# A decoder layer on one core: rows of like TensorE instructions held together, ends of ada blocks issued later

## The chip, the cores and the metric

The program runs on one core of one Trainium2 chip. The metric is the device time of one execution, in microseconds (us), given as the median of several runs. All arithmetic on TensorE (PE) is in FP32 or in pairs of FP32R matmuls; VectorE (DVE), ScalarE (ACT) and GpSimd (POOL) work beside it, and SyncE (SP) issues the weight loads.

## The reference

One layer of a decoder (D = 2048, 256 prompt tokens, 8 x 4 sample tokens, 288 tokens in all):

```
mod = silu(c) @ w_ada + b_ada                    # 9 rows x 6 * 2048: shift, scale, gate, twice
h = rmsnorm(x, g_pre_mix) * (1 + sc_m) + sh_m
q, k, v, gu, gv = split(h @ w_in)                # 1024 | 128 | 128 | 1024 | 1024 columns
attn = sliding-window GQA with sinks and a T5 bias      # 16 heads, 2 kv heads, blocks of 128;
                                                 # sample tokens see a cache of 128 keys each
gmlp = gelu(gu) * (tril(w_s) @ rmsnorm(gelu(gv)) + b_s) # 8 heads, chunks of 128
x = x + gt_m * rmsnorm(concat(rmsnorm(attn), rmsnorm(gmlp)) @ w_out)
h = rmsnorm(x, g_pre_ff) * (1 + sc_f) + sh_f
x = x + gt_f * rmsnorm(square(relu(h @ w_ff1)) @ w_ff2)
```

Outputs are x, the new rows of k and v, and the normalised v rows of the gMLP.

## The kernel before

Activations lie transposed: 128 channels on the partitions, 288 tokens in the columns, 16 such blocks (k = 0..15) for D. Each is kept as a high and a low part (xh, xl), and a weight unit that SP has loaded into a `raw` buffer (five buffers, one queue, one unit after another) is split into h (ACT, L321) and l (DVE, L322). A product is then three matmuls of 128x288 on the full 128 by 128 array: xh by h, xl by h, xh by l (L336, L337, L340; L485, L486, L488 for w_in; L924 for slabs of w_out and w_ff1).

The ada product has nine rows only. It is done in FP32 straight from the raw unit: four matmuls, each of the nine columns of silu(c) against 512 columns (256 or 128 in narrow blocks), stand in four 32-column strips of the array (L363), so four consecutive ones can run beside each other: a pack. In the profile an FP32 matmul leaves two records, a pack of four eight records. A wide block takes four units of one pack each, then its end: ACT copies the sums to `adS` (L367), PE turns it with four transposes (L375), DVE reduces and stores it (L377 to L387).

Other small work on parts of the array: scores of a pair of heads (L531, L532, 64 rows each), the three transposes of the probabilities (L567) and P V of the pair (L572 with 256 and L575 with 128 columns, 64-column halves, two run as a pack), for sample tokens the scores against the cache (L604, eight of 64x32 per kv set), the transposes (L631, L632) and P V (L638, L643), in the gate the transposes of gv (L675, L676) and two products per head (L730, L731).

`items` is a list of work in the order of the program: Win groups of w_in with ada units between; the last group with attention, sample attention and the start of the gate (`do`, at a priority raised by HP = 50 positions); the o slab with the gates; w_out's other units (Main) with groups of three ada units; the residual with norm (`resid`, raised by 60); the f1 slab; the feed-forward. A scheduler gives each engine its order: it takes the ready instruction of the highest priority, by its own estimate of when data is there. So instructions of one step can be pulled apart, and others slipped between. Before, nothing holds the matmuls of a step together. `behind(i, others)` adds a pure ordering to it. `na(n)` hands out the next n ada units in front of which a place in `items` stands, and takes a block's end along straight behind its last unit; `group`, for the later stretch, already puts off an end to the next group.

Of the kernel before, what the change touches and what calls it, by code (L numbers as in the profile page):

```python
# [19 lines left out]
KT = D // 128  # L20
NP = 256
NB = 8
NT_S = 4
NS = NB * NT_S
# [7 lines left out]
KG0 = tuple(sum(KG[:i]) for i in range(len(KG)))  # L32

HP = 50
GTAB = 1
LA, SA = 4, 1
TAILS = ((0, 2), (2, 2), (4, 2), (6, 4), (10, 3), (13, 2), (15, 1))
# [68 lines left out]
def build():  # L106
# [32 lines left out]
    with tile.TileContext(nc) as tc, ExitStack() as root:  # L139
# [10 lines left out]
        V, S, PE, G = nc.vector, nc.scalar, nc.tensor, nc.gpsimd  # L150
# [4 lines left out]
        def behind(ins, others):  # L155
            for o_ in others:
                tc.add_manual_dep(ins, o_.name, mybir.DependencyInfo(mybir.DependencyClass.NoSync,
                                                                     mybir.DependencyReason.DATA),
                                  reason="table order")

        def tracked(i):
            behind(i, order["prev"] if order["load"] is None else [order["load"]])
# [27 lines left out]
        ident = sm("ident")  # L190
# [8 lines left out]
        sc = cp.tile([128, KT, 32], F32, name="sc")  # L199
# [99 lines left out]
        class Unit:  # L299
            src = None  # L300
            cols = 2 * HALF
            n = HALF
# [43 lines left out]
        class Ada(Unit):  # L346
# [7 lines left out]
            def run(self):  # L354
                w, cw = self.w, 128 * self.w
                if self.i == 0:
                    st["ada", self.blk] = pa.tile([128, 512], F32, name="ada")
                ps = st["ada", self.blk]
                nk = KT // w
                for kk in range(nk):  # L360
                    k = self.i * nk + kk
                    g = 32 * (k % 4)
                    PE.matmul(ps[g:g + 32, :cw], sc[:, k], self.raws[:, kk * cw:kk * cw + cw], start=k < 4,  # L363
                              stop=k >= KT - 4, skip_group_check=True)
                if self.i == w - 1:
                    sb = cp.tile([128, 512], F32, name="adS", bufs=2)
                    S.copy(sb[:, :cw], ps[:, :cw])  # L367
                    st["ada", self.blk] = sb

        def ada_fin(blk):  # L370
            c, j0, w = blk
            sb = st["ada", blk]
            pt = pa.tile([128, 512], F32, name="ada")
            for q in range(w):
                PE.transpose(pt[:, q * 128:q * 128 + 128], sb[:, q * 128:q * 128 + 128], ident)  # L375
# [132 lines left out]
        vN = ap_.tile([128, 2, 128], F32, name="vN")  # L508
# [13 lines left out]
        def attn1(i):  # L522
# [2 lines left out]
            G.dma_start(bias[:, :, 0:128], bass.AP(er.tensor, i * EW, [[1, 128], [8 * EW, 2], [1, 128]]))  # L525
            L = bias
            kR = st["kR"]
            for hf in range(2):
                p0 = 64 * hf
                ps = pp.tile([128, 512], F32, name="ps")  # L530
                PE.matmul(ps[:, 0:128], at[p0:p0 + 64, i, 0:128], kR[p0:p0 + 64, 128:256], start=True, stop=True)  # L531
                PE.matmul(ps[:, 128:384], at[p0:p0 + 64, i, 128:256], kR[p0:p0 + 64, 0:256], start=True, stop=True)  # L532
# [27 lines left out]
        def attn2(i):  # L560
            L = st[i]
            pT = []
            for hf in range(2):
                pT.append(ap_.tile([128, 384], F32, name="pT", bufs=2))
                ps = pp.tile([128, 512], F32, name="ps")
                for q, to in ((0, 0), (2, 1), (1, 2)):
                    PE.transpose(ps[:, to * 128:to * 128 + 128], L[:, hf, q * 128:q * 128 + 128], ident)  # L567
                S.copy(pT[hf], ps[:, :384])
            po = pp.tile([128, 512], F32, name="ps")
            for hf in range(2):  # L570
                p0 = 64 * hf
                PE.matmul(po[p0:p0 + 64, 0:256], vN[:, 1, p0:p0 + 64], pT[hf][:, 0:256], start=True, stop=False)  # L572
            for hf in range(2):
                p0 = 64 * hf
                PE.matmul(po[p0:p0 + 64, 128:256], vN[:, 0, p0:p0 + 64], pT[hf][:, 256:384], start=False, stop=True)  # L575
            V.tensor_copy(at[:, i, 0:256], po[:, 0:256])

        def samp0(h):
# [7 lines left out]
        def samp1(h):  # L586

            ck = st["ck"]
# [5 lines left out]
            st["vS"] = vS  # L594
            L = sp.tile([128, 2, 144], F32, name="Ls", bufs=1)
            pss = [pp.tile([128, 512], F32, name="ps") for _ in range(2)]
            for kv in range(2):
                p0 = 64 * kv
                PE.matmul(pss[kv][:, 128:144], qS[p0:p0 + 64, 4 * h:4 * h + 4].rearrange("p b c -> p (b c)"),
                          kT[p0:p0 + 64, n0:n0 + 16], start=True, stop=True)  # L600
            for b in range(4):
                for kv in range(2):
                    p0 = 64 * kv
                    PE.matmul(pss[kv][32 * b:32 * b + 32, 0:128], qS[p0:p0 + 64, 4 * h + b], ck[p0:p0 + 64, b],  # L604
                              start=True, stop=True)
            for kv in range(2):
                V.scalar_tensor_tensor(L[:, kv], pss[kv][:, 0:144], 0.125, biasS[:, kv], ALU.mult, ALU.add)
# [17 lines left out]
        def samp2(h):  # L625
            L, cv, vS = st["Ls"], st["cv"], st["vS"]
            pT = sp.tile([128, 2, 128], F32, name="pTs", bufs=1)
            pN = sp.tile([16, 2, 128], F32, name="pNs", bufs=1)
            psT = pp.tile([128, 512], F32, name="ps").rearrange("p (a c) -> p a c", a=4)
            for kv in range(2):  # L630
                PE.transpose(psT[:, kv], L[:, kv, 0:128], ident)  # L631
                PE.transpose(psT[:16, 2 + kv], L[:, kv, 128:144], ident)  # L632
            S.copy(pT, psT[:, 0:2])
            S.copy(pN, psT[:16, 2:4])
            po = pp.tile([128, 512], F32, name="ps")[:, :128].rearrange("p (b c) -> p b c", b=4)
            for kv in range(2):
                p0 = 64 * kv
                PE.matmul(po[p0:p0 + 64].rearrange("p b c -> p (b c)"), vS[:, p0:p0 + 64], pN[:, kv], start=True,  # L638
                          stop=False, skip_group_check=True)
            for b in range(4):  # L640
                for kv in range(2):
                    p0 = 64 * kv
                    PE.matmul(po[p0:p0 + 64, b], cv[:, b, p0:p0 + 64], pT[:, kv, 32 * b:32 * b + 32], start=False,  # L643
                              stop=True, skip_group_check=True)
# [6 lines left out]
        gm = {}  # L651
# [19 lines left out]
        def gvnat(h):  # L671
            vG, vGs = gm["vG"], gm["vGs"]
            ps = pp.tile([128, 512], F32, name="ps")
            for q in range(2):
                PE.transpose(ps[:, q * 128:q * 128 + 128], gv[:, h][:, q * 128:q * 128 + 128], ident)  # L675
            PE.transpose(ps[:NS, 256:384], gv[:, h][:, NP:], ident)  # L676
# [48 lines left out]
        def gate(h):  # L725
            vG, vGs = gm["vG"], gm["vGs"]
            bs = gm["bs"][:, h]
            ps = pp.tile([128, 512], F32, name="ps")[:, :T]
            for q in range(2):
                PE.matmul(ps[:, q * 128:q * 128 + 128], vG[:, q, h], gm["ws"][:, h], start=True, stop=True)  # L730
            PE.matmul(ps[:, NP:], vGs[:, h], gm["wss"][:, h], start=True, stop=True)  # L731
            t = gv[:, h]
            V.scalar_tensor_tensor(t[:, :NP].rearrange("p (q c) -> p q c", q=2),
                                   ps[:, :NP].rearrange("p (q c) -> p q c", q=2), sm("gvg", h),
# [61 lines left out]
        adas = []  # L796
# [4 lines left out]
        for b in ADA_BLOCKS:  # L801
            if b[0] == 5:
                adas2 += ada_items(b)

        def na(n):
            out = []
            while adas and n > 0:
                it = adas.pop(0)
                out.append(it)
                n -= it.src is not None  # L810
            if adas and adas[0].src is None:
                out.append(adas.pop(0))
            return out

        last = [Win(pc) for pc in WIN_PIECES if pc[0] == len(KG) - 1]

# [152 lines left out]
        def ev_bo():  # L969
            for n in range(NO):  # L970
                ev_o(n)(bo[n][:, :T])

        late = []

        def group(src, n):

# [227 lines left out]
```

## Time and profile before

| | |
|---|---|
| median of 3 runs | 1317.36 us (1317.17 to 1321.53) |
| profiled execution | 1320.14 us, of it 1318.4 us are its span |
| PE busy | 1286.0 us, 98% |
| DVE, ACT, POOL busy | 735.3, 540.0, 36.1 us |
| L363 of 128x512 | 576 records, 76.1 us |
| PE waits for adS L367 / sums L1006 | 5.0 / 3.2 us |

Busy time is time in which at least one instruction of the engine is in flight; a matmul's end is modelled, and consecutive ones overlap, so what a piece of work costs PE is read from start to start. Records named xN are N instructions in a row. "128*32" is the part of the array that an instruction uses (rows by columns), "128x512" its moving operand. In order listings of the program the names carry buffer numbers, and "x3" counts instructions (one per FP32 matmul).

### The profile page before, as it was taken

To read this page: it belongs to the slowest core of one execution; us is meant where nothing else is said; L and a number is where in the kernel's file an instruction comes from. 1 tells how busy PE (TensorE), PEld (TensorE's weight loads), DVE (VectorE), ACT (ScalarE), POOL (GpSimd) and SP (SyncE) were. 2 spreads that over 40 slices of the span, in tenths; PEclk is the share of its full clock that TensorE was granted. 3 is DMA by queue.
4 is the path that set the end of the run, shared out by engine and by line. 5 is a ranking of instruction groups with operands and counts; after the bars stand their busy time and mean duration, and the time that the engine had idled before them with its cause. 6 is when DMAs were issued, how large, how long until landed. Compare 5 with 4: busy or idle time off the path is not lost.

```text
span 1318.4 us, 23358 instructions
## 1 busy us (share of the span) xinstructions
PE 1286.0 (98%) x9770; PEld 1177.8 (89%) x9770; DVE 735.3 (56%) x1407; ACT 540.0 (41%) x873; POOL 36.1 (3%) x59
## 2 busy tenths in 40 slices
PE   6999999999999999999999999999999999999997
PEld 5788886767788689999999889999999999999996
DVE  5888676667644696543334445444544444545554
ACT  4333234466323365443334333334443334444331
POOL 0210001211000000000000000000000000000000
PEclk9999999999999999999999999999999999999999
DMA  9888977677978775544446776445444445544411
GB/s 358 328 312 311 339 285 263 178 285 253 356 319 318 280 264 192 164 166 173 170 160 256 273 291 266 160 160 170 174 168 160 160 160 168 175 169 160 160 65 72
DMA packets 46010, 291.40 MB, mean 221 GB/s; under 512 B 5834, under 2 KB 6410, under 8 KB 15056
## 3 DMA queue, kind: packets, MB, share of 16 engines
q1 hardware_dynamic: 43344, 284.26, 58.6%
q0 software_dynamic: 2416, 5.47, 1.9%
q8 instruction: 76, 1.25, 0.4%
q14 instruction: 30, 0.25, 0.1%
q10 hardware_dynamic: 144, 0.18, 0.0%
HBM read 287.18 MB, written 2.70 MB: 220 GB/s over the span
## 4 chain that ended last, share of the span: by engine, by line
PE 60%; DVE 1%; ACT 0%; DVEq 0%; issue 0%
PE ps L336 20%; PE ps L340 20%; PE ps L337 19%; PE ada L363 1%; DVE acc L1086 0%; DVE x L1092 0%; PE ada L375 0%; PE ps L1083 0%; ACT nr L166 0%; PE ps L270 0%; PE ps L264 0%; DVE mn L214 0%; DVE mn L215 0%; DVE nr L216 0%; DVE mn L224 0%; DVEq L139 0%
## 5 line engine op out<-in xcount | busy, mean ns | idle before, releaser
L322 DVE TENSOR_TENSOR l<-raw,h 128x1024 fp32r<-128x1024 f32 (+3 forms) x368 | 416.3, 1140 | 294.0 <-ACT h L321 291.4
L321 ACT CAST h<-raw 128x1024 fp32r<-128x1024 f32 (+3 forms) x368 | 357.7, 984 | 500.5 <-PE ps L337 410.0
L336 PE MATMUL ps<-xh,h 128*128 128x288 f32 x1120 | 301.8, 297 | 1.7 <-ACT h L321 1.0
L337 PE MATMUL ps<-xl,h 128*128 128x288 f32 x1120 | 301.1, 295 | 0.0
L337 PE MATMUL ps<-fl,h 128*128 128x288 f32 x1024 | 276.9, 295 | 0.0
L336 PE MATMUL ps<-fh,h 128*128 128x288 f32 x1024 | 276.9, 298 | 0.0
L336 PEld LDWEIGHTS ps<-xh,h 128*128 128x128 f32 x1120 | 210.4, 188 | 7.0 <-ACT h L321 5.3
L337 PEld LDWEIGHTS ps<-xl,h 128*128 128x128 f32 x1120 | 211.6, 189 | 0.8 <-issue 0.8
L336 PEld LDWEIGHTS ps<-fh,h 128*128 128x128 f32 x1024 | 193.0, 188 | 0.0
L337 PEld LDWEIGHTS ps<-fl,h 128*128 128x128 f32 x1024 | 192.2, 188 | 0.0
L340 PE MATMUL ps<-xh,l 128*128 128x288 f32 x1120 | 171.7, 295 | 0.0
L340 PE MATMUL ps<-fh,l 128*128 128x288 f32 x1024 | 157.3, 296 | 0.0
L340 PEld LDWEIGHTS ps<-xh,l 128*128 128x128 f32 x1120 | 156.1, 188 | 0.0
L340 PEld LDWEIGHTS ps<-fh,l 128*128 128x128 f32 x1024 | 142.7, 188 | 0.0
L485 PE MATMUL ps<-xh,h 128*128 128x288 f32 x416 | 118.6, 308 | 4.3 <-ACT xh L292 2.3
L486 PE MATMUL ps<-xl,h 128*128 128x288 f32 x416 | 117.7, 301 | 0.0
L363 PE MATMUL ada<-raw,sc 128*32 128x512 f32 (+2 forms) x1088 | 104.4, 480 | 7.4 <-DMA raw<-wada 7.4
L485 PEld LDWEIGHTS ps<-xh,h 128*128 128x128 f32 x416 | 78.5, 192 | 18.5 <-issue 6.3
L488 PE MATMUL ps<-xh,l 128*128 128x288 f32 x416 | 87.2, 301 | 0.0
L486 PEld LDWEIGHTS ps<-xl,h 128*128 128x128 f32 x416 | 79.8, 192 | 2.6 <-issue 2.4
L363 PEld LDWEIGHTS ada<-raw,sc 128*32 128x32 f32 x1088 | 31.4, 112 | 44.8 <-issue 31.7
L488 PEld LDWEIGHTS ps<-xh,l 128*128 128x128 f32 x416 | 66.6, 192 | 1.1 <-issue 1.0
(255 smaller groups left out, 931.9 us busy)
## 6 DMA issues: line engine op xcount, KB each, us to landing
raw<-wada SPq DMA_DIRECT2D x96, 1024.0 KB, 7.4
raw<-f SPq DMA_DIRECT2D x64, 1024.0 KB, 4.8
raw<-f1B SPq DMA_DIRECT2D x58, 1024.0 KB, 4.8
raw<-woB SPq DMA_DIRECT2D x12, 1024.0 KB, 9.2
raw<-win SPq DMA_DIRECT2D x11, 1024.0 KB, 8.7
raw<-win SPq DMA_DIRECT2D x14, 640.0 KB, 4.8
raw<-f1A SPq DMA_DIRECT2D x8, 768.0 KB, 7.2
raw<-win SPq DMA_DIRECT2D x6, 768.0 KB, 5.9
```

The lines of the kernel that those rows point to most:

```text
L321: S.copy(h, rw)
L322: V.tensor_tensor(l, rw, h.bitcast(F32), ALU.subtract)
L336: PE.matmul(ps, w, self.mh[:, k], start=k == 0, stop=False)
L337: PE.matmul(ps, w, self.ml[:, k], start=False, stop=False)
L340: PE.matmul(ps, l[:, kk * 128:kk * 128 + 128], self.mh[:, k], start=False, stop=k == 15)
L363: PE.matmul(ps[g:g + 32, :cw], sc[:, k], self.raws[:, kk * cw:kk * cw + cw], start=k < 4, stop=k >= KT - 4, skip_group_check=True)
L485: PE.matmul(ps, w, xh[:, k0 + kk], start=kk == 0, stop=False)
L486: PE.matmul(ps, w, xl[:, k0 + kk], start=False, stop=False)
L488: PE.matmul(ps, l[:, o_ + kk * 128:o_ + kk * 128 + 128], xh[:, k0 + kk], start=False, stop=kk == s - 1)
```

## The change

A class Row is added. The first instruction of a row is issued as before; each later one is issued at a priority raised by 20000 positions and ordered behind the one ahead of it, so that once the first is placed, the rest follow at once. Rows are: the four matmuls of an ada unit (eight or sixteen in narrow blocks); the transposes of an ada end; the four score matmuls of a pair; the three transposes of each half; the four P V matmuls of a pair, with half 1 now ahead of half 0; the ten score matmuls of a sample set; its four transposes, small ones first; its ten P V matmuls; the three transposes of a gv head; the three matmuls of a gate. And `na` puts a block's end behind the units of its next call, as `group` does; `late` moves ahead of it.

```diff
+TOP = 20000
+        class Row:
+            prev = None
+
+            def __call__(self, f, *a, **kw):
+                if self.prev is None:
+                    i = f(*a, **kw).ins
+                else:
+                    with tc.high_priority(offset=TOP):
+                        i = f(*a, **kw).ins
+                    behind(i, [self.prev])
+                self.prev = i
+                return i
...
+                row = Row()
                 for kk in range(nk):
...
-                    PE.matmul(ps[g:g + 32, :cw], sc[:, k], self.raws[:, kk * cw:kk * cw + cw], start=k < 4,
-                              stop=k >= KT - 4, skip_group_check=True)
+                    row(PE.matmul, ps[g:g + 32, :cw], sc[:, k], self.raws[:, kk * cw:kk * cw + cw], start=k < 4,
+                        stop=k >= KT - 4, skip_group_check=True)
...
             po = pp.tile([128, 512], F32, name="ps")
-            for hf in range(2):
+            row = Row()
+            for hf in (1, 0):
                 p0 = 64 * hf
-                PE.matmul(po[p0:p0 + 64, 0:256], vN[:, 1, p0:p0 + 64], pT[hf][:, 0:256], start=True, stop=False)
-            for hf in range(2):
+                row(PE.matmul, po[p0:p0 + 64, 0:256], vN[:, 1, p0:p0 + 64], pT[hf][:, 0:256], start=True, stop=False)
+            for hf in (1, 0):
...
+            row = Row()
             for kv in range(2):
                 p0 = 64 * kv
-                PE.matmul(pss[kv][:, 128:144], qS[p0:p0 + 64, 4 * h:4 * h + 4].rearrange("p b c -> p (b c)"),
+                row(PE.matmul, pss[kv][:, 128:144], qS[p0:p0 + 64, 4 * h:4 * h + 4].rearrange("p b c -> p (b c)"),
                           kT[p0:p0 + 64, n0:n0 + 16], start=True, stop=True)
             for b in range(4):
                 for kv in range(2):
                     p0 = 64 * kv
-                    PE.matmul(pss[kv][32 * b:32 * b + 32, 0:128], qS[p0:p0 + 64, 4 * h + b], ck[p0:p0 + 64, b],
+                    row(PE.matmul, pss[kv][32 * b:32 * b + 32, 0:128], qS[p0:p0 + 64, 4 * h + b], ck[p0:p0 + 64, b],
...
+            row = Row()
             for q in range(2):
-                PE.matmul(ps[:, q * 128:q * 128 + 128], vG[:, q, h], gm["ws"][:, h], start=True, stop=True)
-            PE.matmul(ps[:, NP:], vGs[:, h], gm["wss"][:, h], start=True, stop=True)
+                row(PE.matmul, ps[:, q * 128:q * 128 + 128], vG[:, q, h], gm["ws"][:, h], start=True, stop=True)
+            row(PE.matmul, ps[:, NP:], vGs[:, h], gm["wss"][:, h], start=True, stop=True)
...
+        late = []
+
         def na(n):
-            out = []
+            out, ends = [], list(late)
+            late.clear()
             while adas and n > 0:
                 it = adas.pop(0)
-                out.append(it)
-                n -= it.src is not None
+                if it.src is None:
+                    ends.append(it)
+                else:
+                    out.append(it)
+                    n -= 1
             if adas and adas[0].src is None:
-                out.append(adas.pop(0))
-            return out
+                late.append(adas.pop(0))
+            return out + ends
```

What it does to PE's order, at three places. In the listings of after, L169 is the first instruction of a row and L172 any later one; the names tell what it is (ck, qS: sample scores; bias: transposes of probabilities; pT, vN: P V; raw, sc: ada; adS, ones: sums of squares; small, adS: transposes of an ada end).

The first place is the scores of the first sample set (about 212 us in the trace). PE before, where ps_2623 and ps_2624 are the two score tiles:

```order
L567 MATMUL ps_2652<-small_75,bias_2354 128x128 x3
L604 MATMUL ps_2623<-ck_654,qS_122 32x128
L567 MATMUL ps_2658<-small_75,bias_2354 128x128
L604 MATMUL ps_2624<-ck_654,qS_122 32x128
L567 MATMUL ps_2658<-small_75,bias_2354 128x128
L604 MATMUL ps_2623<-ck_654,qS_122 32x128
L567 MATMUL ps_2658<-small_75,bias_2354 128x128
L604 MATMUL ps_2624<-ck_654,qS_122 32x128
L572 MATMUL ps_2663<-pT_2651,vN_125 64x256
```

PE after:

```order
L172 MATMUL ps_2623<-ck_654,qS_122 32x128
L172 MATMUL ps_2624<-ck_654,qS_122 32x128
L172 MATMUL ps_2623<-ck_654,qS_122 32x128
L172 MATMUL ps_2624<-ck_654,qS_122 32x128
L172 MATMUL ps_2623<-ck_654,qS_122 32x128
L172 MATMUL ps_2624<-ck_654,qS_122 32x128
L172 MATMUL ps_2623<-ck_654,qS_122 32x128
L172 MATMUL ps_2624<-ck_654,qS_122 32x128
L169 MATMUL ps_2652<-small_75,bias_2354 128x128
L172 MATMUL ps_2652<-small_75,bias_2354 128x128 x2
L169 MATMUL ps_2658<-small_75,bias_2354 128x128
L172 MATMUL ps_2658<-small_75,bias_2354 128x128 x2
```

The eight cache scores now stand in a row behind the two of the new keys, and the six transposes behind them; before, transposes, P V and scores of a head pair came between.

The second place is ada units between the last attention pairs (about 250 us). PE before, where raw_3022 and raw_3079 are two units:

```order
L363 MATMUL ada_3170<-raw_3022,sc_95 32x512 x3
L363 MATMUL ada_3170<-raw_3079,sc_95 32x512
L572 MATMUL ps_3331<-pT_3319,vN_125 64x256
L531 MATMUL ps_3343<-kR_2347,at_121 128x128
L532 MATMUL ps_3343<-kR_2347,at_121 128x256
L531 MATMUL ps_3347<-kR_2347,at_121 128x128
L532 MATMUL ps_3347<-kR_2347,at_121 128x256
L572 MATMUL ps_3331<-pT_3325,vN_125 64x256
L575 MATMUL ps_3331<-pT_3319,vN_125 64x128
L575 MATMUL ps_3331<-pT_3325,vN_125 64x128
L363 MATMUL ada_3170<-raw_3079,sc_95 32x512 x3
L363 MATMUL ada_3170<-raw_3096,sc_95 32x512 x4
```

PE after, with the units raw_3022 to raw_3159 of one stretch (raw_3302 follows as the sixth):

```order
L169 MATMUL ada_3161<-raw_3022,sc_95 32x512
L172 MATMUL ada_3161<-raw_3022,sc_95 32x512 x3
L169 MATMUL ada_3161<-raw_3079,sc_95 32x512
L172 MATMUL ada_3161<-raw_3079,sc_95 32x512 x3
L169 MATMUL ada_3161<-raw_3087,sc_95 32x512
L172 MATMUL ada_3161<-raw_3087,sc_95 32x512 x3
L169 MATMUL ada_3194<-small_75,adS_3085 128x128
L172 MATMUL ada_3194<-small_75,adS_3085 128x128 x3
L169 MATMUL ada_3161<-raw_3123,sc_95 32x512
L172 MATMUL ada_3161<-raw_3123,sc_95 32x512 x3
L169 MATMUL ada_3363<-raw_3159,sc_95 32x512
L172 MATMUL ada_3363<-raw_3159,sc_95 32x512 x3
```

The units are no longer cut by score and P V matmuls, and six of them stand with one ada end between them; the two Win units that were loaded ahead of raw_3302 come after it on PE.

The third place is the residual (about 450 us). PE before, where L245 are its sums of squares:

```order
L245 MATMUL ps_5089<-adS_5092,ones_80 128x288 x2
L245 MATMUL ps_5089<-adS_5098,ones_80 128x288 x2
L245 MATMUL ps_5089<-adS_5104,ones_80 128x288 x2
L245 MATMUL ps_5089<-adS_5110,ones_80 128x288 x2
L245 MATMUL ps_5089<-adS_5116,ones_80 128x288 x2
L245 MATMUL ps_5089<-adS_5122,ones_80 128x288 x2
L245 MATMUL ps_5089<-adS_5128,ones_80 128x288 x2
L245 MATMUL ps_5089<-adS_5134,ones_80 128x288 x2
L375 MATMUL ada_5174<-small_75,adS_5172 128x128 x4
L363 MATMUL ada_5193<-raw_5147,sc_95 32x512 x4
L363 MATMUL ada_5193<-raw_5154,sc_95 32x512 x4
L363 MATMUL ada_5193<-raw_5160,sc_95 32x512 x4
```

PE after, where they are L261:

```order
L169 MATMUL ada_5184<-raw_5147,sc_95 32x512
L172 MATMUL ada_5184<-raw_5147,sc_95 32x512 x3
L169 MATMUL ada_5184<-raw_5154,sc_95 32x512
L172 MATMUL ada_5184<-raw_5154,sc_95 32x512 x3
L261 MATMUL ps_5089<-adS_5092,ones_80 128x288 x2
L261 MATMUL ps_5089<-adS_5098,ones_80 128x288 x2
L261 MATMUL ps_5089<-adS_5104,ones_80 128x288 x2
L261 MATMUL ps_5089<-adS_5110,ones_80 128x288 x2
L169 MATMUL ada_5184<-raw_5160,sc_95 32x512
L172 MATMUL ada_5184<-raw_5160,sc_95 32x512 x3
L261 MATMUL ps_5089<-adS_5116,ones_80 128x288 x2
L261 MATMUL ps_5089<-adS_5122,ones_80 128x288 x2
```

Two units of the last block stand ahead of the sums now and one more behind the eighth; the two ends, ahead and behind the last four units before, both stand at the end, just ahead of the f1 slab. SP's order of loads is the same in both programs.

## Rows read from the trace of the kernel before

**Rows 1.** PE's share and the granted clock in 40 slices: the page, whole span.
```profile
PE 1286.0 (98%) x9770; PEld 1177.8 (89%) x9770; DVE 735.3 (56%) x1407; ACT 540.0 (41%) x873; POOL 36.1 (3%) x59
...
PEclk9999999999999999999999999999999999999999
```

**Rows 2.** PE's waits by releaser: us in total, times, longest us; whole span.
```profile
PE ada L363 <- DMA raw<-wada: 7.4, 3, 6.7
PE ada L375 <- ACT adS L367: 5.0, 7, 2.0
PE ps L245 <- ACT adS L1006: 3.2, 4, 1.7
...
PE ps L731 <- POOL vGs L710: 0.6, 1, 0.6
```

**Rows 3.** PE's timeline, four ada units on end (start us, us, line, out<-in, records).
```profile
698.24 3.64 PE L363 MATMUL ada<-raw,sc 128*32 128x512 f32 x32
701.81 0.40 PE L336 MATMUL ps<-xh,h 128*128 128x288 f32 x1
```

**Rows 4.** PE's timeline, one ada matmul alone, behind a wait.
```profile
224.08 0.66 PE L375 MATMUL ada<-small,adS 128*128 128x128 f32 x4 [2.03 <-ACT adS L367]
...
225.30 1.04 PE L363 MATMUL ada<-raw,sc 128*32 128x512 f32 x2
226.27 0.43 PE L638 MATMUL ps<-pNs,vS 16*64 16x128 f32 x2
```

**Rows 5.** PE's timeline: a P V pack alone; a row of P V packs.
```profile
251.77 0.65 PE L572 MATMUL ps<-pT,vN 128*64 128x256 f32 x2
252.35 0.50 PE L531 MATMUL ps<-kR,at 64*128 64x128 f32 x4
...
253.21 0.43 PE L572 MATMUL ps<-pT,vN 128*64 128x256 f32 x1
...
254.01 2.77 PE L363 MATMUL ada<-raw,sc 128*32 128x512 f32 x22
```

**Rows 6.** PE's timeline, sample scores, transposes and P V in turn.
```profile
212.21 0.40 PE L604 MATMUL ps<-ck,qS 64*32 64x128 f32 x2
212.55 0.33 PE L567 MATMUL ps<-small,bias 128*128 128x128 f32 x1
212.81 0.40 PE L604 MATMUL ps<-ck,qS 64*32 64x128 f32 x2
...
216.67 0.41 PE L604 MATMUL ps<-ck,qS 64*32 64x128 f32 x4
217.01 0.43 PE L575 MATMUL ps<-pT,vN 128*64 128x128 f32 x2
217.37 0.40 PE L604 MATMUL ps<-ck,qS 64*32 64x128 f32 x2
```

**Rows 7.** PE's timeline, an ada end behind another wait.
```profile
330.96 0.66 PE L375 MATMUL ada<-small,adS 128*128 128x128 f32 x4 [0.70 <-ACT adS L367]
```

**Rows 8.** Two stretches: us, busy us by engine, clock, DMA share.
```profile
180.00:240.00 60.00, 57.41 (x408) 43.28 (x407) 41.52 (x134) 25.95 (x77) 5.07 (x8) 1.00 0.68 230
...
445.00:468.00 23.00, 18.60 (x108) 9.21 (x108) 19.76 (x45) 10.86 (x20) 0.00 (x0) 1.00 0.57 220
```

**Rows 9.** DMA issues of 278 to 279.5 us: KB each, us to landing.
```profile
raw<-wada SPq DMA_DIRECT2D x1, 1024.0 KB, 5.5
raw<-win SPq DMA_DIRECT2D x1, 640.0 KB, 3.8
```

**Rows 10.** PE's timeline, first sums of the residual, and the f1 slab.
```profile
451.30 2.21 PE L245 MATMUL ps<-adS,ones 128*128 128x288 f32 x8 [1.73 <-ACT adS L1006]
...
467.54 1.07 PE L924 MATMUL ps<-xh,h 128*128 128x288 f32 x6
```

**Rows 11.** Two stretches near the start: a gap, then half clock.
```profile
53.00:55.40 2.40, 0.43 (x9) 0.02 (x1) 2.40 (x7) 0.00 (x0) 0.00 (x0) 1.00 1.05 375
55.40:58.70 3.30, 3.30 (x14) 3.30 (x15) 2.94 (x8) 0.41 (x1) 1.42 (x3) 0.51 1.00 419
```

More of the change, by code (lines that the diff above doesn't have):

```diff
@@ L373, in ada_fin @@
             pt = pa.tile([128, 512], F32, name="ada")
+            tr = Row()
             for q in range(w):
-                PE.transpose(pt[:, q * 128:q * 128 + 128], sb[:, q * 128:q * 128 + 128], ident)
+                tr(PE.transpose, pt[:, q * 128:q * 128 + 128], sb[:, q * 128:q * 128 + 128], ident)
             m = cp.tile([128, 4, 9], F32, name="adm", bufs=2)[:, :w]
@@ L527, in attn1 @@
             kR = st["kR"]
+            qk = Row()
             for hf in range(2):
@@ L530, in attn1 @@
                 ps = pp.tile([128, 512], F32, name="ps")
-                PE.matmul(ps[:, 0:128], at[p0:p0 + 64, i, 0:128], kR[p0:p0 + 64, 128:256], start=True, stop=True)
-                PE.matmul(ps[:, 128:384], at[p0:p0 + 64, i, 128:256], kR[p0:p0 + 64, 0:256], start=True, stop=True)
+                qk(PE.matmul, ps[:, 0:128], at[p0:p0 + 64, i, 0:128], kR[p0:p0 + 64, 128:256], start=True, stop=True)
+                qk(PE.matmul, ps[:, 128:384], at[p0:p0 + 64, i, 128:256], kR[p0:p0 + 64, 0:256], start=True, stop=True)
                 V.scalar_tensor_tensor(L[:, hf], ps[:, :384], 0.125, bias[:, hf], ALU.mult, ALU.add)
@@ L565, in attn2 @@
                 ps = pp.tile([128, 512], F32, name="ps")
+                tr = Row()
                 for q, to in ((0, 0), (2, 1), (1, 2)):
-                    PE.transpose(ps[:, to * 128:to * 128 + 128], L[:, hf, q * 128:q * 128 + 128], ident)
+                    tr(PE.transpose, ps[:, to * 128:to * 128 + 128], L[:, hf, q * 128:q * 128 + 128], ident)
                 S.copy(pT[hf], ps[:, :384])
             po = pp.tile([128, 512], F32, name="ps")
-            for hf in range(2):
+            row = Row()
+            for hf in (1, 0):
                 p0 = 64 * hf
-                PE.matmul(po[p0:p0 + 64, 0:256], vN[:, 1, p0:p0 + 64], pT[hf][:, 0:256], start=True, stop=False)
-            for hf in range(2):
+                row(PE.matmul, po[p0:p0 + 64, 0:256], vN[:, 1, p0:p0 + 64], pT[hf][:, 0:256], start=True, stop=False)
+            for hf in (1, 0):
                 p0 = 64 * hf
-                PE.matmul(po[p0:p0 + 64, 128:256], vN[:, 0, p0:p0 + 64], pT[hf][:, 256:384], start=False, stop=True)
+                row(PE.matmul, po[p0:p0 + 64, 128:256], vN[:, 0, p0:p0 + 64], pT[hf][:, 256:384], start=False, stop=True)
             V.tensor_copy(at[:, i, 0:256], po[:, 0:256])
@@ L629, in samp2 @@
             psT = pp.tile([128, 512], F32, name="ps").rearrange("p (a c) -> p a c", a=4)
+            tr = Row()
             for kv in range(2):
-                PE.transpose(psT[:, kv], L[:, kv, 0:128], ident)
-                PE.transpose(psT[:16, 2 + kv], L[:, kv, 128:144], ident)
+                tr(PE.transpose, psT[:16, 2 + kv], L[:, kv, 128:144], ident)
+            for kv in range(2):
+                tr(PE.transpose, psT[:, kv], L[:, kv, 0:128], ident)
             S.copy(pT, psT[:, 0:2])
             S.copy(pN, psT[:16, 2:4])
+            row = Row()
             po = pp.tile([128, 512], F32, name="ps")[:, :128].rearrange("p (b c) -> p b c", b=4)
@@ L637, in samp2 @@
                 p0 = 64 * kv
-                PE.matmul(po[p0:p0 + 64].rearrange("p b c -> p (b c)"), vS[:, p0:p0 + 64], pN[:, kv], start=True,
+                row(PE.matmul, po[p0:p0 + 64].rearrange("p b c -> p (b c)"), vS[:, p0:p0 + 64], pN[:, kv], start=True,
                           stop=False, skip_group_check=True)
@@ L642, in samp2 @@
                     p0 = 64 * kv
-                    PE.matmul(po[p0:p0 + 64, b], cv[:, b, p0:p0 + 64], pT[:, kv, 32 * b:32 * b + 32], start=False,
+                    row(PE.matmul, po[p0:p0 + 64, b], cv[:, b, p0:p0 + 64], pT[:, kv, 32 * b:32 * b + 32], start=False,
                               stop=True, skip_group_check=True)
@@ L673, in gvnat @@
             ps = pp.tile([128, 512], F32, name="ps")
+            tr = Row()
             for q in range(2):
-                PE.transpose(ps[:, q * 128:q * 128 + 128], gv[:, h][:, q * 128:q * 128 + 128], ident)
-            PE.transpose(ps[:NS, 256:384], gv[:, h][:, NP:], ident)
+                tr(PE.transpose, ps[:, q * 128:q * 128 + 128], gv[:, h][:, q * 128:q * 128 + 128], ident)
+            tr(PE.transpose, ps[:NS, 256:384], gv[:, h][:, NP:], ident)
             S.copy(vG[:, :, h], ps[:, :256].rearrange("p (q c) -> p q c", q=2))
@@ L728, in gate @@
             ps = pp.tile([128, 512], F32, name="ps")[:, :T]
+            row = Row()
             for q in range(2):
-                PE.matmul(ps[:, q * 128:q * 128 + 128], vG[:, q, h], gm["ws"][:, h], start=True, stop=True)
-            PE.matmul(ps[:, NP:], vGs[:, h], gm["wss"][:, h], start=True, stop=True)
+                row(PE.matmul, ps[:, q * 128:q * 128 + 128], vG[:, q, h], gm["ws"][:, h], start=True, stop=True)
+            row(PE.matmul, ps[:, NP:], vGs[:, h], gm["wss"][:, h], start=True, stop=True)
             t = gv[:, h]
@@ L971, in ev_bo @@
                 ev_o(n)(bo[n][:, :T])
-        late = []
         def group(src, n):
```

## The prediction

> **What bounds the kernel now.** I read the page first: PE is busy for 1286.0 of 1318.4 us and the clock stands at full speed in every fortieth of the span [rows 1]. So the time is the length of PE's queue, and a change that leaves the arithmetic alone can save only in what PE loses between instructions. There are two kinds of that. One is waits, and the list of PE's waits shows how few there are: 5.0 us for the copies that end an ada block, 3.2 us for the sums of the residual, 7.4 us for the first loads [rows 2]. The other does not look like a loss: "busy" time in which part of the array is used, or in which the pipeline changes from one use to another. It is read from start to start in the timeline. Four ada units on end take 3.57 us to the next matmul, 0.89 per pack of four [rows 3]. One single matmul of a pack, cut off from the others, takes 0.97 [rows 4]: more than the four. A single sample score takes 0.34 and a single transpose between two of them 0.26 [rows 6]. So each time a step is cut in two, the second piece costs about what the whole does. All of this lies before 470 us; the feed-forward behind it has no small work but three ada blocks that are whole in both programs.
>
> **What the rows save.** I counted in PE's order of both programs how often each kind of work stands in one piece (a pack is a set of neighbours on different parts of the array).
> Ada of 128x512: 79 packs become 72. Seven times 0.97 [rows 4] is 6.8 us. Narrower units lose three packs, about 1.2 us with their switches, an estimate at under half of the wide price each. Together 8.0.
> P V of a pair: 15 packs of 256 columns and 12 of 128 become 8 and 8, always one behind the other. Such a row stands in before by chance: from 253.21 to 254.01 it takes 0.80 us [rows 5]; eight of them are 6.4. A pack of 256 alone takes 0.58 [rows 5], one of 128 0.36 [rows 6]; 15 and 12 of them are 13.0, less some 0.9 for those that had neighbours already: 12.1. Saved 5.7.
> Sample scores: 13 pieces become two rows of eight. 13 times 0.34 [rows 6] is 4.4. No row of eight is in the trace. The piece at 216.67 has two (four records) and takes 0.34 too, so a second one costs nothing. If only twos overlap, a row takes four times 0.34, both rows 2.7; if all eight overlap, little over 0.34 each and 0.9 for both. Saved 1.7 to 3.5; I take 3.0, since the eight use eight different parts of the array, as the two do.
> The Trainium skill (TensorE: Matmul & The Clock Gate, Part 3) gives a pack the span of one matmul and some 4 ns for each further tile; by that the two rows would take about 0.7 and save 3.7.
> Transposes: 59 stretches become 46, single ones 23 become 12. Four on end take 0.66 with the last one's tail [rows 4], so inside a stretch one costs about 0.13, and a stretch joined to another saves 0.13 to 0.26 [rows 6]: 13 times that is 1.7 to 3.4; I take 2.8, nearer the upper end, since the lost ones mostly stood alone between tiled work.
> Sample P V: 16 packs become 10; at 0.26 [rows 6], the cheapest single piece, 1.5 us.
> Pair scores: in two of eight pairs a transpose stood inside; each is two changes of use at 0.26 [rows 6], 1.0 in all.
> Gate: its small product stood four times behind several large ones and now stands behind each head's two, three more changes of use, each an estimate of 0.2 by the 0.26 of a transpose: 0.5 lost.
> The sum is 8.0 + 5.7 + 3.0 + 2.8 + 1.5 + 1.0 - 0.5 = 21.5 us, all on PE's queue and so on the path, with 18 and 23.5 as its bounds.
>
> **What the later ends save.** The transposes of an ada end wait for ACT's copy. At 224.08 that is 2.03 us [rows 4], at 330.96 another 0.70 [rows 7]. Units now stand between a block's last matmul and its end, so both go: 2.7 us. The waits at the start are not touched, and the one at 467 lies in a stretch where PE would wait for the norm anyway [rows 10]. So 24.2 us in all if nothing else happened.
>
> **What it costs.** Four places.
> First, loads. SP's queue keeps its order, and there are five raw buffers. At the second place shown above six ada units are used nearly in a row, and the sixth was issued behind two Win units that PE uses after it. The buffers of these two and of the sixth come free when the first, second and third of the six are used. From a free buffer a unit of 640 KB takes 3.8 us to landing, 1 MB behind such units 5.5 us [rows 9]. The sixth is issued as the third ends, an ada end (0.5) and two units (1.8) before its turn: 5.5 less 2.3, PE waits about 3.2 us. Before, the Win units stood in between and no such wait is in the list [rows 2]. I take 3.5 for this and smaller ones (the stretches of units 65 to 71 and 130 to 135 have five in a row); bounds 0 and 8. What is queued behind the waiting unit is all of PE, and through it the splits.
> Second, attention. DVE is busy for 41.5 of 60 us between 180 and 240 [rows 8], and a row of P V starts only when the copy of the second half's transposes is there, while the 24 transposes of gv stand in one block. Each of eight pairs can lose some 0.2 to 0.5 us for ACT; work of w_in stands between most of them. I take 2, bounds 0 and 6.
> Third, the gate. POOL's and DVE's chain to vGs is late by 0.6 us now [rows 2], and PE reaches it with less work in between: 1 us, bounds 0 and 2.
> Fourth, the residual. Its length is set by DVE and ACT: DVE is busy for 19.8 of 23 us [rows 8], the sums come in bursts that wait for ACT, the first at 451.30, and the f1 slab starts at 467.54 [rows 10]. The eight units of the last two blocks were hidden in this. Now two of the last four stand ahead of the first sum and two between the sums, 0.9 us each, and the sixth of them needs the buffer of the first (it lands 5 to 6 us after that was used, two late). The chain slips by about 2 us, and with a second copy and further splits on ACT and DVE I take 2.5, bounds 0 and 5. What these units leave behind, the stretch before the f1 slab, becomes idle time.
> Together 3.5 + 2 + 1 + 2.5 = 9 us. Net 24.2 - 9 = 15.2. The profiled execution was 1320.1 (1318.4 of span and 1.7 around it), 2.8 over the median; a difference of spans carries over, so I put it on the median: 1317.4 - 15.2 = 1302.
>
> **Rivals.** (A) The loads take more. If each of the three stretches of five or six units waits for one whole load of 5.5 us [rows 9], that is 16.5 instead of 3.5, and the time is 1315; with half of it 1309. For it: 0.68 DMA share between 180 and 240 [rows 8] rises as PE gets faster, and buffers are held by units that come later. Against: PE has no wait for a load in before behind the first ones [rows 2].
> (B) It ends slower: rows turn PE into a follower of the softmax chain. Each pair's P V row waits for its transposes and ACT's copy of them, with only a piece of w_in between. The clock adds to it: the gap of 1.97 us at 53.4 was followed by 3.3 us at 0.51, the half speed of 1.2 GHz [rows 11], which cost 1.7 us. If each of eight pairs waited 1.8 us and lost 1.7 to the clock, that is 28 us in place of the 2 counted, and 1317.4 - 24.2 + 7 + 28 = 1328. It decides at (24.2 - 7) / 8, 2.2 us per pair with the clock: above that the kernel is slower than before. Against: at present pairs lose nothing, and in the new order w_in stands between transposes and P V.
> The Trainium skill (TensorE: Matmul & The Clock Gate, HAM oscillation) describes this loop of a wait that drops the clock, and expects it where short work alternates with waits of microseconds; between 180 and 240 us the trace shows 1.00 throughout.
> (C) It doesn't do what it says: the pieces that I count as lone already overlap more than the starts show, or the rows run no faster on end. Then half of 21.5 is left, and the time is 1313. Against: the row at 253.21 [rows 5].
> (D) None of the costs comes, since all lie beside other work: 1317.4 - 24.2 = 1293.
>
> **How the numbers follow.** The forecast, 1302 with 1296 to 1308 by the bounds of the costs taken together: 0.55. (A) 0.20, half of it above 1310.8. (B) 0.08, (C) 0.08, most of it within 0.5%. (D) 0.09. A measurement of this kernel tells some 0.5% (6.6 us) from no change. Faster, under 1310.8: 0.55 + 0.09 + 0.10 + 0.05 = 0.79; same: 0.14; slower: 0.07. The range leaves out the lower part of (D), the upper of (A), and (B): 1294 to 1313.
>
> **What would show it right or wrong.** L604 with two pieces only and L363 of 128x512 at some 69 us instead of 76; from 180 to 300 us nearly 18 us shorter; the feed-forward from the f1 slab on as long as before. A new line "PE ada L363 <- DMA" of 3 us near 240 us shows the loads; more than 8 us there is (A). Gaps ahead of P V rows of over 1 us, with PEclk under 1, are (B). An idle stretch of some 5 us before the f1 slab belongs to the forecast; if the clock falls there, 1.7 us are to be added. If L363, P V, scores and transposes together are less than 12 us shorter, (C) holds.

## The result and the profile after

The changed kernel takes 1311.75 us (median of 11 runs, 1311.0 to 1315.7) against 1317.84 of the kernel before: a ratio of 0.9949, interval 0.9937 to 0.9961. It is faster by 6.1 us; forecast were 15.2. The profiled executions differ by more, 1320.1 and 1311.1 us, spans 1318.4 and 1309.4.

The page of after, PE's share and the clock in 40 slices, answers to [rows 1]; the list of PE's waits (us in total, times, longest us) to [rows 2]:

```profile
PE 1268.9 (97%) x9770; PEld 1174.8 (90%) x9770; DVE 736.3 (56%) x1407; ACT 541.3 (41%) x873; POOL 38.0 (3%) x59
...
PEclk9999999989999899999999999999999999999999
```

```profile
PE ada L169 <- DMA raw<-wada: 14.8, 4, 6.7
PE ada L169 <- ACT adS L384: 3.5, 4, 2.4
PE ps L957 <- ACT xh L308: 2.8, 1, 2.8
...
PE ps L169 <- ACT vGs L704: 1.8, 1, 1.8
```

PE is busy for 17 us less, but its share has fallen, two slices have lost clock, and three new waits stand in the list: for a load (14.8 in place of 7.4), for the norm ahead of the f1 slab, and for ACT's copies of gv.

The rows themselves do what was said of them. PE's timeline, the first sample set and a pair behind it (start us, us, line, records), answers to [rows 5] and [rows 6]:

```profile
205.71 0.45 PE L172 MATMUL ps<-ck,qS 64*32 64x128 f32 x16
206.09 0.33 PE L169 MATMUL ps<-small,bias 128*128 128x128 f32 x1
...
207.59 0.43 PE L169 MATMUL ps<-pT,vN 128*64 128x256 f32 x1
...
208.38 0.37 PE L169 MATMUL ps<-kR,at 64*128 64x128 f32 x1
```

Eight scores (16 records) take 0.38 us to the next instruction, where one alone took 0.34; the P V row of a pair takes 0.79.

What came instead is seen in three stretches. PE's timeline at the 24 transposes of gv (the idle time and its releaser stand in brackets):

```profile
244.42 0.33 PE L169 MATMUL ps<-small,gv 128*128 128x128 f32 x1 [0.74 <-DVE gv L515]
...
246.78 0.45 PE L169 MATMUL ps<-small,gv 128*128 128x128 f32 x1 [1.81 <-ACT vGs L704]
```

PE's timeline at the six ada units:

```profile
261.25 0.60 PE L172 MATMUL ada<-raw,sc 128*32 128x512 f32 x3
267.88 1.06 PE L169 MATMUL ada<-raw,sc 128*32 128x512 f32 x1 [6.02 <-DMA raw<-wada]
```

PE's timeline at the end of the residual, answering to [rows 10]:

```profile
438.43 4.27 PE L261 MATMUL ps<-adS,ones 128*128 128x288 f32 x16
...
451.82 0.47 PE L169 MATMUL ada<-small,adS 128*128 128x128 f32 x1 [2.42 <-ACT adS L384]
...
455.76 1.57 PE L957 MATMUL ps<-xh,h 128*128 128x288 f32 x5 [2.82 <-ACT xh L308]
```

The stretches around them (us, busy us of PE, PEld, DVE, ACT, POOL, granted clock, DMA share, GB/s):

```profile
247.00:261.00 14.00, 13.99 (x110) 9.13 (x113) 9.11 (x30) 7.79 (x27) 1.44 (x2) 0.88 0.33 80
261.00:267.80 6.80, 0.86 (x8) 0.00 (x0) 2.71 (x13) 6.77 (x17) 0.00 (x0) 0.72 0.97 341
267.80:271.00 3.20, 3.12 (x13) 1.47 (x14) 2.12 (x4) 2.90 (x5) 2.40 (x2) 0.50 0.95 347
271.00:275.00 4.00, 4.00 (x22) 3.98 (x21) 3.04 (x9) 0.73 (x1) 2.95 (x2) 0.60 0.88 335
...
455.80:459.20 3.40, 3.40 (x14) 3.40 (x15) 2.95 (x14) 1.39 (x4) 0.00 (x0) 0.50 0.08 34
459.20:463.00 3.80, 3.80 (x22) 3.80 (x21) 2.96 (x12) 2.10 (x6) 0.00 (x0) 0.65 0.00 0
```

Behind each of the three PE works on at half speed, 1.2 GHz, for some microseconds: time in these rows times the clock that is missing gives 1.7 + 1.6 + 1.6 + 1.7 + 1.3 = 7.9 us. In the profile of before the same sum is 3.2, behind the two gaps near the start [rows 11]; in this execution of after the two gaps there, of 2.0 us each, were not followed by half speed.

So the span's account, with PE's instructions summed from start to start and gaps taken apart:

| us | before | after | difference | forecast |
|---|---|---|---|---|
| PE's instructions | 1285.6 | 1268.6 | -17.0 | |
| of it lost at half speed | 3.2 | 7.9 | +4.7 | 0 |
| PE's instructions at full speed | 1282.4 | 1260.7 | -21.7 | -21.5 |
| gaps between them | 17.8 | 25.7 | +7.9 | +6.3 |

### The profile page after: what moved, and what is told of

The parts are those of the page before. It is cut to its first block, busy times and chain, and to the rows that moved or that the text cites. A ratio compares the mean times of both kernels' runs of the same rounds, so it can differ in the third digit from the quotient of the medians.

```text
span 1309.4 us, 23367 instructions
## 1 busy us (share of the span) xinstructions
PE 1268.9 (97%) x9770; PEld 1174.8 (90%) x9770; DVE 736.3 (56%) x1407; ACT 541.3 (41%) x873; POOL 38.0 (3%) x59
## 4 chain that ended last, share of the span: by engine, by line
PE 61%; DVE 1%; ACT 0%; DVEq 0%; issue 0%
PE ps L352 20%; PE ps L356 20%; PE ps L353 20%; PE ada L169 1%; DVE acc L1117 0%; DVE x L1123 0%; PE ada L172 0%; PE ps L1114 0%; ACT nr L182 0%; PE ps L286 0%; PE ps L280 0%; DVE mn L230 0%; DVE nr L232 0%; DVE mn L231 0%; DVE mn L240 0%; DVEq L140 0%
## 5 line engine op out<-in xcount | busy, mean ns | idle before, releaser
L169 PE MATMUL ada<-raw,sc 128*32 128x512 f32 (+2 forms) x192 | 82.9, 544 | 15.0 <-DMA raw<-wada 14.8
L172 PE MATMUL ada<-raw,sc 128*32 128x512 f32 (+2 forms) x896 | 96.6, 471 | 0.0
```

Of the source, the lines that this page charges most:

```text
L169: i = f(*a, **kw).ins
L172: i = f(*a, **kw).ins
```

## Experiments

Every ratio is to the kernel before, which was run again beside each experiment; its median moves between 1317.6 and 1318.6 us. After was not run again. The four experiments that are compared with after here were faster in every run than after in any, but by the intervals the sizes of these differences are uncertain by some 2 to 3 us.

**What the load wait hangs on, and what the clock costs.** Theory: ada units that PE takes last hold the five raw buffers, loads stop, and PE later waits; each such gap is then followed by half speed, which is paid on top. The SP queue of after speaks for the first half (raw loads by start; none is issued between 236.8 and 257.8 us, and the DMA share above is 0.33):

```profile
234.76 2.06 SPq L326 DMA_DIRECT2D raw<-wada  x2
257.76 1.19 SPq L326 DMA_DIRECT2D raw<-win  x2
259.48 1.91 SPq L326 DMA_DIRECT2D raw<-wada  x2
```

A stop alone need not cost anything, though. In before the queue issues no load from 257.7 to 274.9 us, and no wait for a load follows:

```profile
251.89 5.76 SPq L310 DMA_DIRECT2D raw<-wada  x5
274.90 3.56 SPq L310 DMA_DIRECT2D raw<-win  x2
```

```profile
279.72 0.40 PE L485 MATMUL ps<-xh,h 128*128 128x288 f32 x1
```

There PE comes to the first of the new loads at 279.7, 4.8 us after its issue. In after, PE is free at 261.9, 4.1 us after the queue moves on, and what it wants then is not the first new load but the third (the sixth ada unit). That one was issued at 259.48 and is used at 267.88, 8.4 us later.

Rival: it is the later ends alone, which put six units in a row. Two edits, one for each:

```diff
+                elif self.prev is None:
+                    with tc.high_priority(offset=self.hp):
+                        i = f(*a, **kw).ins
...
+                if self.c in (2, 3, 4):
+                    row.hp = 60
```

> The changed kernel with the first matmul of each ada unit of the second kind (blocks handed out by na and group) at a priority raised by 60, so that a unit runs as soon as it is there and does not stand behind attention; by PE's order they then stand singly between pieces of w_in and attention, never over two in a row before 260 us, at about 2.7 us more of PE work for switches. Theory 1 (five buffers held by ada units that PE takes last stop the loads from 247 to 258 us, and so cause the wait of 6.0 us and the half clock behind): loads go on, the wait and the half clock there are gone, 6 to 7 us faster than the changed kernel: 1304 to 1307. Rival (the wait is that of the split behind gelu on ACT, or of DMA bandwidth): PE waits 4 us or more near 265 us all the same, 1310 to 1315.

Measured: 1306.6 us, ratio 0.9909 (0.9891 to 0.9928), inside the theory's range, though 5.1 us under after and not 6 to 7. Of the waits for loads 8.4 are left at the start and 1.7 in the residual; new is a gap of 2.7 us ahead of an o slab. From 243 to 275 us the clock is full and the loads go on:

```profile
243.00:258.00 15.00, 14.01 (x110) 10.43 (x109) 10.47 (x34) 11.77 (x42) 2.46 (x3) 1.00 0.93 360
258.00:275.00 17.00, 16.82 (x131) 10.67 (x129) 13.79 (x45) 13.97 (x33) 3.09 (x3) 1.00 0.64 222
```

The other edit gives `na` its old form, `out.append(it)`, `n -= it.src is not None`, ends taken along at once, and leaves all rows:

> The changed kernel with na as before, so the ends of ada blocks come straight behind their last unit again; all rows stay. Theory 1: the late ends are what put six ada units in a row at 260 us; here four, a piece of w_in, an end and one: the load wait there falls from 6.0 to under 3 us, the half clock behind it is shorter; the waits for adS of some 2.7 us come back; the block of 24 transposes of gv still waits 2.5 us; time 1307 to 1311. Rival (the late ends are worth their 2.7 us and the loads wait the same): 1313 to 1315.

Measured: 1309.0 us, 0.9928 (0.9914 to 0.9941), as expected in time. The wait at this place is not shorter, it has another name. The wait of this kernel, its load of that Win unit (issue; KB, us to landing), and its ACT timeline ahead of the end of the gap at 270.92:

```profile
PE ps L503 <- ACT h L337: 7.6, 2, 7.0
```

```profile
261.36 1.19 SPq L326 DMA_DIRECT2D raw<-win  x2
```

```profile
raw<-win SPq DMA_DIRECT2D x1, 640.0 KB, 3.8
```

```profile
266.10 1.28 ACT L188 ACT_TABLE_LOAD   x1
267.40 1.91 ACT L185 ACTIVATE gv<-gv 128x2048 f32<-128x2048 f32 x1
269.21 1.04 ACT L185 ACTIVATE vGs<-vGs 32x1024 f32<-32x1024 f32 x1
270.16 1.96 ACT L337 CAST h<-raw 128x640 fp32r<-128x640 f32 x3
```

PE has no sixth ada unit ahead of w_in here and waits 7.0 us for the split of the Win unit. Its load was late too, but it had landed at 265.2; then the table load and the gelu, 266.1 to 270.2, stood ahead of the split on ACT. Without these two the split could have begun at 266.1, 4 us earlier; by that estimate some 3 us of the wait are the load's, near what the theory said, and 4 are the gelu's, as the first edit's rival said. So it is not the later ends alone: loads that come late after the stop make whoever comes next wait, and how long depends on the order on PE and on ACT.

The clock was tested by filling gaps with matmuls that change no result (24 add zeros to the ada sums, 10 and 12 write to a spare bank; two of the three places are shown):

```diff
+                if self.i == 1 and self.blk == adas_blks[3]:
+                    row.prev = fill(24, st["lastA"], ps)
...
+            if blk == adas_blks[-1]:
+                tr.prev = fill(10, st["lastT"])
```

> The changed kernel with matmuls of no use in two of its waits: 24 (zeros added to the ada sums, about 5.2 us) between the fifth and the sixth ada unit at 261 us, 10 and 12 (into a spare bank) before and behind the last ada end ahead of the f1 slab. The loads, DVE and ACT stay as they are, so the waits keep their ends; only PE's idle time is filled. Theory 1 (the clock at half speed behind these waits costs 5 to 6 us): the granted clock stays at 1.0 behind 268 us and in the f1 slab, the first ada units and 2 us of matmuls run at full speed: 1305 to 1308. Rival (the waits alone are the loss, what ran at half clock was waiting for something else too): 1311 to 1313.

Measured: 1307.6 us, 0.9913 (0.9899 to 0.9928); the loads are no earlier. The fill and the ada unit behind it, and the clock in three stretches:

```profile
263.70 5.62 PE L172 MATMUL ada<-zer,small 128*128 128x128 f32 x48
269.25 1.06 PE L172 MATMUL ada<-raw,sc 128*32 128x512 f32 x8
```

```profile
247.00:261.00 14.00, 13.33 (x94) 9.58 (x94) 8.20 (x27) 7.52 (x27) 1.44 (x2) 0.77 0.20 35
...
268.00:275.00 7.00, 6.65 (x51) 5.39 (x51) 4.20 (x8) 5.36 (x8) 4.48 (x2) 1.00 0.94 337
454.00:461.00 7.00, 6.54 (x51) 6.35 (x50) 7.00 (x33) 5.15 (x13) 0.00 (x0) 1.00 0.25 90
```

Work without use in idle time made the kernel 4.2 us faster. Half speed behind these two gaps comes to 1.6 + 1.6 + 1.7 + 1.3 = 6.2 us by the rows of after. The fill's profile loses 1.5 us more than after behind the gap at gv, which was not filled: the clock is 0.77 from 247 to 261 us, 0.88 in after. So 4.2 us probably understates what half speed behind the two gaps cost.

**The residual.** The last block's units are ordered behind the last sum again, `row.prev = st["lastS"]` for them:

> The changed kernel with the four units of the last ada block ordered behind the last of the residual's sums, as the kernel before had them; both ends stay behind them. Theory (two and more units among the sums delay the chain by some 2 us, and the idle stretch of 2.4 and 2.8 us that they leave behind halves the clock of the f1 slab): the sums wait for ACT by some 3 us again, the f1 slab starts 2 us earlier than in the changed kernel, no gap over 1.5 us stands just ahead of it and the clock there stays at 1.0: 4 to 5 us faster than the changed kernel, 1306.5 to 1308.5. Rival (the slab is bound by the norm chain on DVE and ACT wherever the units stand, and the clock falls with either gap): 1310.5 to 1312.5.

Measured: 1306.4 us, 0.9898 (0.9875 to 0.9922), 5.3 us under after. The end of the residual in this kernel, and the clock behind its first sum and ahead of the slab:

```profile
439.57 7.94 PE L261 MATMUL ps<-adS,ones 128*128 128x288 f32 x24 [2.58 <-ACT adS L1042]
...
449.82 3.64 PE L172 MATMUL ada<-raw,sc 128*32 128x512 f32 x32
...
455.07 1.07 PE L962 MATMUL ps<-xh,h 128*128 128x288 f32 x6 [0.25 <-ACT xh L308]
```

```profile
439.40:442.90 3.50, 3.33 (x7) 2.47 (x8) 3.50 (x7) 1.47 (x3) 0.00 (x0) 0.51 0.98 398
449.00:456.00 7.00, 6.63 (x51) 3.08 (x50) 6.49 (x20) 4.65 (x11) 0.00 (x0) 1.00 0.57 212
```

From the residual's first sum over the columns (L280, at 431.62 in after and 433.52 here) to the slab it is 24.1 us in after and 21.6 here, and the clock stays at 1.00 ahead of the slab. Behind the gap of 2.58 us it falls here too, but among the sums, which in before waited for ACT between their bursts: the four bursts take 10.2 us here and 10.3 in before. The four units cover the norm's chain; pulled ahead, they delay it and leave a gap.

**The parts one by one.** Before with rows for ada units and ends alone, with those of attention, samples and gate alone, and with the later ends alone:

> Before with rows for ada units and ada ends alone; na and all other steps as before. By PE's order the ada packs of 512 columns go from 79 to 72 and transposes are cut less often. Theory 1 (the rows save what was counted; the changed kernel gives it back in waits and at half clock): about 9 to 10 us of PE work less, the transposes of gv are in two blocks with w_in between, no load wait over 2 us, clock 0.995 or more: ratio to before 0.992 to 0.994. Theory 2 (a cut pack costs less than its start to start time says, the gain of rows is small by itself): ratio 0.997 to 1.0.

> Before with the rows of attention, samples and gate alone; ada units, ada ends and na as before. By PE's order 11.4 us of PE work less. Theory 1: the 24 transposes of gv in one block wait for ACT's copies by 2 to 3 us and the clock falls behind them, other waits take 1 to 4 us more near the gelu: ratio 0.994 to 0.997. Rival (the rows give what was counted): ratio 0.991 to 0.992.

> Before with the later ends of na alone, no rows. The prediction put 2.7 us of saved waits on this part, less the slip at the residual of 2.5. Theory 1: the waits of 2.0 and 0.7 us for adS go, PE's order costs about 1 us more in switches, the residual loses 2 to 5 us with the clock: ratio 1.000 to 1.003. Rival (the ends are a gain by themselves): ratio 0.998 or less.

Small rows: 0.9945 (0.9925 to 0.9965), 1311.6 us, as expected in time but not in mechanism. The 24 transposes of gv stand in one block and do not wait; PE waits for a load instead, and the clock behind is at half speed:

```profile
271.83 1.92 PE L379 MATMUL ada<-raw,sc 128*32 128x512 f32 x2 [4.20 <-DMA raw<-wada]
```

```profile
271.80:276.50 4.70, 4.67 (x14) 3.01 (x15) 3.06 (x5) 3.00 (x6) 3.34 (x2) 0.50 0.57 239
```

So the load wait needs neither the rows of ada units nor the later ends. Ada rows: 0.9981 (0.9963 to 0.9999), a miss of theory 1 by 5 to 8 us, and a time inside the range of theory 2. Its twelve runs reach from 1309.9 us at a mean clock of 0.997 to 1321.1 at 0.985. In the profiled one PE waits 2.0 us up to 218.3 and then works for 19 us at half speed, through the small work of the attention stretch and, from 235.1 us, w_in:

```profile
221.00:228.00 7.00, 7.00 (x33) 3.29 (x29) 0.28 (x1) 0.96 (x2) 1.41 (x2) 0.50 0.62 251
228.00:240.00 12.00, 12.00 (x57) 8.61 (x56) 5.09 (x20) 2.11 (x9) 0.56 (x1) 0.51 0.26 53
```

That is 9.4 us lost there. PE's instructions take 1281.7 us from start to start in this profile; less the 9.4 that is 1272.3, against 1282.4 at full speed in before: some 10 us are saved, as theory 1 said, and in this execution the clock takes them back. Three runs keep the clock, 0.996 or 0.997, and take 1309.9 to 1311.3.
Later ends alone: 1331.3 us, 1.0089 (1.0068 to 1.011), much worse than either theory. The waits for adS are gone but for 1.4 us; in their place stand 5.4 us for a load from 278.2, 2.3 ahead of an o slab and 5.5 ahead of the f1 slab:

```profile
PE ps L930 <- ACT xh L292: 5.5, 1, 5.5
PE ps L930 <- ACT xh L280: 2.3, 1, 2.3
```

**Both remedies, and less.** Early units with the held block; early units with all rows and the old `na`; and the first of these with twelve matmuls of no use ahead of the fifth o slab:

> The changed kernel with both remedies: the first matmul of an ada unit at a raised priority (as in e4_early) and the last block's units behind the sums of the residual (as in e5_resid). Theory: the two act at different places and add up: 1306.6 less 4 to 5, 1301 to 1303. Rival (the time saved at one place is lost to the next wait or to the clock): 1305 to 1307.

> All rows of the change, na as before (no later ends), and the first matmul of an ada unit at a raised priority. By PE's order 16.3 us of work less than before (2.5 less than e8_early_resid has saved), the residual's last block stands behind the sums without being held. Theory (the rows are the gain, the later ends bring nothing that early units do not): 1301 to 1304, as e8_early_resid within 3 us. Rival (the later ends are needed for the waits on adS once units run early): 1306 or more.

> e8_early_resid with 12 matmuls of no use (2.6 us, into a spare bank) ahead of the fifth o slab, where PE waits 2.7 us for xh and then runs 48 matmuls in 8.3 us instead of 6.4. Theory (a gap of this length halves the clock behind it, and that costs as much again): the gap is filled, PEclk stays at 1.0 behind 317 us, 1.5 to 2.5 us faster than e8_early_resid: 1298.5 to 1299.5. Rival (the 48 matmuls are slow for another reason): 1300.5 to 1302.

Measured: 1301.0 us, 0.9860 (0.9836 to 0.9885); 1300.2 us, 0.9865 (0.9846 to 0.9883); 1299.4 us, 0.9853 (0.9835 to 0.9870). The two remedies add up. The later ends are not needed: the kernel without them is as fast. The last one shows the clock once more in its profile (its 1.6 us in the medians are not clear of noise); 48 matmuls of the o slab took 8.3 us behind a gap of 2.7 [first row, kernel with both remedies] and 6.6 behind the filled one [second row]:

```profile
317.30:324.00 6.70, 6.70 (x37) 6.50 (x38) 5.52 (x13) 3.47 (x8) 0.00 (x0) 0.75 0.87 364
```

```profile
318.00:324.00 6.00, 6.00 (x50) 4.63 (x48) 5.91 (x13) 4.08 (x9) 0.00 (x0) 1.00 1.02 430
```

All three beat both kernels, by about 17 to 18 us against before.

## Why the prediction was wrong

The time lies inside the range, near its upper end, but the forecast gain of 15.2 us is 2.5 times the measured one, 9.1 us too much. By the account above, 4.7 of these are the clock in the profiles, 1.6 are gaps, and 2.9 come from going from the profile to the median, which is the clock again; the rows gave 0.2 the other way. By its own steps:

- **What bounds it, and what the rows save**: right. 21.5 was forecast, 21.7 measured at full speed. By kind: P V 5.7 (5.7 forecast), sample scores 3.6 (3.0), ada 7.1 with some units at half speed in it, 8.0 without (8.0), transposes 2.9 at full speed (2.8), sample P V 1.7 (1.5), pair scores 1.0 (1.0), gate -0.6 (-0.5).
- **What the later ends save**: wrong in sign. The waits of 2.0 and 0.7 us for adS went, but the units that moved there lengthened other waits: alone they cost 11.7 us by the ratio, and taken out of the changed kernel they gave 2.8.
- **Loads**: the place was right, the size and the reason were not. Forecast were 3.5 for all such waits, 3.2 of it here; measured 6.0 here and 2.0 at two others, 1.5 of it in the residual, where the prediction had seen a buffer come free late. The issue (as the third of the six ends) and the lead (2.3 us forecast, 2.4 measured) came true. Mis-sized is the landing: 5.5 us was read from a unit behind one other load [rows 9]; the sixth is the third of five loads that were issued within 4.2 us, and took 8.4.
- **Attention**: 2 forecast, 2.6 measured (0.7 stood there before), but in the block of gv transposes and not at P V, whose rows hardly wait.
- **Gate**: 1 forecast; the wait for vGs is 0.4 (0.6 before), and 0.5 and 0.9 come new behind it, ahead of a sum of squares and of an o slab.
- **Residual**: 2.5 forecast, 1.9 measured to the f1 slab.
- **The gaps together**: 6.3 more forecast, 7.9 measured. That they came so near is partly luck: the waits for loads grew by 7.4 us where 3.5 stood, and a wait of 1.0 us for a split, which the forecast did not count, went away.
- **The clock**: the step that failed. Time lost at half speed stands at nothing in the sum, without a reason; it is only in rival (B), behind P V, and as 1.7 us "to be added" at the end. That a gap of 2 us can be followed by half speed was read in [rows 11] and not applied to the 9 us of waits in the forecast. After lost 7.9 us to it, 4.7 more than before. From the f1 slab to the end it took 853.6 us against 850.9, where the prediction said as long as before, and filling two of the three gaps gave 4.2 us. Rival (B) had the right mechanism at the wrong place. The Trainium skill (TensorE: Matmul & The Clock Gate, HAM oscillation) describes a wait for a load behind which the next work runs at the lower clock. Three places here agree in kind, with gaps of 2.6 (0.7 and 1.8), 6.0 and 5.2 us (2.4 and 2.8); two gaps of 2.0 us near the start of the same profile do not.
- **From the profile to the median**: wrong too. The prediction carried a difference of spans over to the median; the profiles differ by 9.0 us, the medians by 6.1. Before's runs at a mean clock of 0.998 or 0.999 take 1316.5 to 1317.6 us, its profiled one at 0.996 took 1320.1 and had lost 3.2 us behind the gaps at the start; that comes in some executions only. A difference of two single executions is not one of medians where the clock moves.

Rival (A) gave 1309 to 1315 for loads alone, and the time lies there; but the waits for loads grew by 7.4 us, less than the 10 to 16.5 that this takes, and the clock made up the rest. That the time is (A)'s and inside the range is luck. (C) and (D) fell.

## What to carry to other kernels

Matmuls that use parts of the array belong side by side: a row held by order saved what a count of packs times the lone start-to-start time said. But a tuned queue hides other chains behind its scattered pieces; before pieces are pulled together, ask which buffers they hold until then, which load PE needs first once loads go on, and which chain the pieces covered. Price a gap together with the half speed that can follow it (here 1.7, 3.2 and 3.0 us behind gaps of 2.6, 6.0 and 5.2), and check with a fill of useless work, which separates the wait from the clock.

## What the runs showed of the hardware

Eight 64x128 score matmuls on eight parts of the array take 0.38 us, one alone 0.34. The clock's fall is not tied to one gap length: gaps of 1.8 and 2.0 us at 21 and 53 us were followed by half speed in the profile of before, and gaps of 2.0 us at the same places in that of after were not. Nor is the time at half speed: in the kernel with ada rows alone the granted clock stood at 0.50 for 19 us, with PE busy throughout, in small work for all but the last 5 us, and behind the three gaps of after for some 3 to 6 us of work. What decides either was not tried and stays open.
